# A first load that begins with one 2 KB descriptor per DMA engine instead of eight

## The chip, the cores and the metric

The kernel runs on one core of a Trainium2 chip. The metric is the device time of one execution in microseconds (us), taken as the median of several executions. All times within a trace count from the start of its span; the time of an execution is about 1.8 us longer than the span. An execution counts as slow when it is over 1.5% above the fastest of the same kernel.

## The reference

Each of the 32 x 3 images of 256 x 256 float32 values is turned by 180 degrees. Seen as a row of 65,536 numbers, an image is simply reversed:

```
x: (32, 3, 256, 256) float32
return np.rot90(x, k=2, axes=(-2, -1))
```

25.17 MB are read and 25.17 MB are written; nothing is calculated.

## The kernel before

The 96 images are handled in three groups of 32 images, one for each of the buffers A, Bt and Ct in SBUF, the memory of the core with its 128 partitions. Each image takes four partitions, so a load is 128 rows of 64 KB (E = 16,384 numbers). DVE, the vector engine, reverses the rows in place, in pieces of J = 2048 columns by way of a buffer T; the store puts the four rows of an image in reverse order. N = 512 columns are 2 KB; the first 2 KB of a row are called a strip here. All transfers are issued from SP, the sync engine, so they stand in one queue, from which 16 DMA engines take their rows. At the end of its share of a load each engine writes to the load's semaphore, a counter for which the next user waits; the last of these writes is the load's landing.

```python
# ... sizes, views, buffers, copy() on DVE and back(), the columns in reverse ...
def load(t, g, lo=0, hi=E):
    nc.sync.dma_start(out=t[:, lo:hi], in_=x4[g][:, lo:hi])

def store(t, g):
    nc.sync.dma_start(out=o4[g][:, ::-1, :], in_=t[:, :])

def inside(t):
    for lo in range(0, E // 2, J):
        hi = E - lo - J
        copy(T[:, :], back(t, hi, hi + J))
        copy(t[:, hi:hi + J], back(t, lo, lo + J))
        copy(t[:, lo:lo + J], T[:, :])

load(A, 0, 0, N)      # 128 strips of 2 KB
load(A, 0, N, E)      # 128 rows of 62 KB
load(Bt, 1)           # 128 rows of 64 KB
load(Ct, 2)
for g, t in enumerate((A, Bt, Ct)):
    inside(t)
    store(t, g)
# ... launch on one core ...
```

## Time and profile before

| what | value |
|---|---|
| time, median of 3 first runs | 122.92 us (122.82 to 123.0) |
| span of the profiled run | 121.1 us |
| DVE busy | 44.2 us |
| DMA packets' time, share of 16 engines | 97.4% |
| traffic | 50.33 MB, 416 GB/s over the span |

The lines themselves are shown and read in the prediction. The trace also records every single packet with its start, duration and size. A packet of 64 KB is one row; where this document speaks of an engine's rows, the numbers come from these records, as the mean of the 16 engines. The records do not name the engine: the n-th rows of all engines are the n-th sixteen long packets in order of their starts.

### The profile page before, as it was taken

What the parts mean: (1) busy time and instruction counts of PE and PEld (TensorE: products, weight loads), DVE (VectorE), ACT (ScalarE), POOL (GpSimd) and SP (SyncE); (2) the same over time, 40 slices, a digit from 0 to 9 for tenths busy, and PEclk for the clock granted to TensorE, in tenths of its full rate; (3) what the DMA queues carried; (4) which work ended last, traced back from release to release, by engine and by line L of the source; (5) the groups of instructions that cost most, each with busy time, mean ns of one, the idle gap of its engine ahead of it and who ended that gap; (6) DMA issues with size and microseconds to landing.
All of it is one profiled execution on the core that took longest, in us unless ns stands there. A gap on an engine that the chain in (4) does not pass through costs nothing.

```text
span 121.1 us, 94 instructions
## 1 busy us (share of the span) xinstructions
DVE 44.2 (36%) x36; POOL 0.2 (0%) x4
## 2 busy tenths in 40 slices
DVE  0000000599994199998039999600000000000000
POOL 0000000000000000000000000000000000000000
DMA  9977987897799879978989977997799779977980
GB/s 359 399 336 336 650 356 336 346 693 346 346 411 628 346 346 476 563 346 346 346 346 476 563 346 346 563 476 346 346 584 455 346 346 606 433 346 346 671 368 0
DMA packets 1008, 50.33 MB, mean 416 GB/s; under 512 B 112, under 2 KB 112, under 8 KB 240
## 3 DMA queue, kind: packets, MB, share of 16 engines
q1 hardware_dynamic: 1008, 50.33, 97.4%
HBM read 25.17 MB, written 25.17 MB: 416 GB/s over the span
## 4 chain that ended last, share of the span: by engine, by line
DMA 33%; DVE 25%; another core or an unknown queue 4%; issue 1%; SPq 1%; DVEq 0%
DMA Bt<-in_x_dram 33%; DVE T L53 8%; DVE Ct L53 8%; DVE Bt L53 8%; SPq L56 1%; DVEq L53 0%
## 5 line engine op out<-in xcount | busy, mean ns | idle before, releaser
L53 DVE COPY T<-A 128x2048 f32<-128x2048 f32 x4 | 4.9, 1227 | 22.7 <-DMA A<-in_x_dram 22.6
L53 DVE COPY T<-Ct 128x2048 f32<-128x2048 f32 x4 | 4.9, 1227 | 5.4 <-DMA Ct<-in_x_dram 5.3
L53 DVE COPY T<-Bt 128x2048 f32<-128x2048 f32 x4 | 4.9, 1227 | 4.4 <-DMA Bt<-in_x_dram 4.3
L53 DVE COPY Bt<-T 128x2048 f32<-128x2048 f32 x4 | 4.9, 1227 | 0.1
L53 DVE COPY A<-T 128x2048 f32<-128x2048 f32 x4 | 4.9, 1227 | 0.1
L53 DVE COPY Ct<-Ct 128x2048 f32<-128x2048 f32 x4 | 4.9, 1227 | 0.1
L53 DVE COPY Bt<-Bt 128x2048 f32<-128x2048 f32 x4 | 4.9, 1227 | 0.1
L53 DVE COPY A<-A 128x2048 f32<-128x2048 f32 x4 | 4.9, 1227 | 0.1
L53 DVE COPY Ct<-T 128x2048 f32<-128x2048 f32 x4 | 4.9, 1227 | 0.1
L89 POOL MEMSET const-bfloat16-1.0<- 128x1 bf16 x1 | 0.1, 101 | 0.0
L89 POOL MEMSET const-uint8-127<- 128x1 uint8 x1 | 0.1, 101 | 0.0
L89 POOL MEMSET const-float32-0.0<- 128x1 f32 x1 | 0.1, 98 | 0.2 <-issue 0.2
L89 POOL MEMSET const-float32-1.0<- 128x1 f32 x1 | 0.1, 98 | 0.0
## 6 DMA issues: line engine op xcount, KB each, us to landing
A<-in_x_dram SPq DMA_DIRECT2D x1, 7936.0 KB, 21.4
A<-in_x_dram SPq DMA_DIRECT2D x1, 256.0 KB, 2.8
Bt<-in_x_dram SPq DMA_DIRECT2D x1, 40.3
Ct<-in_x_dram SPq DMA_DIRECT2D x1, 60.3
out_dram<-A SPq DMA_DIRECT2D x1, 43.9
out_dram<-Bt SPq DMA_DIRECT2D x1, 43.8
out_dram<-Ct SPq DMA_DIRECT2D x1, 42.7
```

The source lines that it names most:

```text
L53: tc.keep_in_program_order(nc.vector.tensor_copy(out=dst, in_=src))
L56: nc.sync.dma_start(out=t[:, lo:hi], in_=x4[g][:, lo:hi])
L89: nc = _bacc.Bacc("TRN2", target_bir_lowering=False, num_devices=1)
```

## The change

The strip in front exists to set the engines to work early. The change makes it as small as it can be, one descriptor for each of the 16 engines, so that the long rows can begin sooner. The other 112 strips follow behind the long rows.

```diff
-    def load(t, g, lo=0, hi=E):
-        nc.sync.dma_start(out=t[:, lo:hi], in_=x4[g][:, lo:hi])
+    def load(t, g, lo=0, hi=E, i=0, j=P):
+        nc.sync.dma_start(out=t[i:j, lo:hi], in_=x4[g][i:j, lo:hi])
...
-    load(A, 0, 0, N)
+    load(A, 0, 0, N, 0, 16)
     load(A, 0, N, E)
+    load(A, 0, 0, N, 16, P)
     load(Bt, 1)
     load(Ct, 2)
```

## The prediction

> **What bounds the kernel now.** I read the page from the top: the busy shares first, then the queue's share, then the chain that ended last, and then, since the change touches only the first microseconds of the transfers, the windows and the single packets there. The page of the kernel before:
>
> ```profile
> span 121.1 us, 94 instructions
> ...
> DVE 44.2 (36%) x36; POOL 0.2 (0%) x4
> ...
> DMA packets 1008, 50.33 MB, mean 416 GB/s; under 512 B 112, under 2 KB 112, under 8 KB 240
> ## 3 DMA queue, kind: packets, MB, share of 16 engines
> q1 hardware_dynamic: 1008, 50.33, 97.4%
> ...
> DMA 33%; DVE 25%; another core or an unknown queue 4%; issue 1%; SPq 1%; DVEq 0%
> ```
>
> The only compute engine that works, DVE, is busy for 44.2 of 121.1 us. The one queue keeps the 16 DMA engines busy for 97.4% of the span. The chain that ended last names DVE for 25%, which misleads: it follows semaphores and not the place in the queue. The issues show this:
>
> ```profile
> A<-in_x_dram SPq DMA_DIRECT2D x1, 7936.0 KB, 21.4
> A<-in_x_dram SPq DMA_DIRECT2D x1, 256.0 KB, 2.8
> ...
> out_dram<-A SPq DMA_DIRECT2D x1, 43.9
> out_dram<-Bt SPq DMA_DIRECT2D x1, 43.8
> ```
>
> Each load or store of 8 MB alone takes about 19.3 us (8.39 MB at 435 GB/s), yet a store lands 43.9 us after its issue: it stands some 24 us behind the loads ahead of it. The store of A is issued at 37.76 us (timeline) and the load of Ct has landed only at about 62.4 us, when DVE begins on Ct. So the vector work has more than 20 us of slack, and the span is: time to the first packet, plus what each DMA engine has to move, plus the end. The windows (us from the start of the span, busy DVE and POOL, clock, DMA share, GB/s) give the same by stage:
>
> ```profile
> 0.00:1.70 1.70, 0.00 (x0) 0.20 (x4) 1.00 0.00 0
> 1.70:2.70 1.00, 0.00 (x0) 0.00 (x0) 1.00 0.75 184
> 2.70:21.80 19.10, 0.00 (x0) 0.00 (x0) 1.00 1.01 430
> 21.80:41.10 19.30, 14.72 (x12) 0.00 (x0) 1.00 1.00 435
> ...
> 119.50:121.10 1.60, 0.00 (x0) 0.00 (x0) 1.00 0.01 0
> ```
>
> Nothing moves until 1.7 us; for a microsecond the engines move the 2 KB strips at 184 GB/s; from there on they run at 430 to 435 GB/s. Only the second row can be improved by this change.
>
> **What the Trainium skill says.** (1) "DMA: Bandwidth & Descriptors", section "Where 436 GB/s comes from", puts the ceiling of the 16 engines together at 435 GB/s; the window from 21.8 to 41.1 us shows 435, so it agrees, and no change of order can speed the bulk. (2) The same page, "Why a DMA increments its semaphore by 16 and not by 1", says that a DMA from the SP queue takes the largest number of engines up to 16 that divides the slowest dimension. So 16 rows go one to each engine, and 112 rows seven to each. Before, every load has 128 rows, and the trace shows 16 landings on each semaphore; 112 rows no run has shown yet. (3) The same page, "Queues, rings and completion order": each engine takes its descriptors in ring order. The packet records agree: on each engine the 62 KB rows follow the strip with no gap. (4) "SBUF — State Buffer", "Door 1: The DMA port swizzle", has 16 ports, shared by eight partitions each in fours, so seven consecutive rows lie on two or three ports. Whether that costs anything is not visible before.
>
> **The change part by part.** The bytes stay the same: 50.33 MB, so 3.146 MB for each of 16 engines. Per engine the records of single packets show for the kernel before: eight strips of 2 KB at 0.084 us each when settled (the first takes 0.08 to 0.62 us, the start-up), a semaphore write of 0.009 us, eight rows of 62 KB at 2.342 us, and forty rows of 64 KB at 2.418 us.
>
> *Removed from the head.* Seven of eight strips, 7 x 0.084 = 0.59 us per engine. The first 62 KB rows now start at 2.71 to 3.18 us, mean 2.95.
>
> *What then sets the start of the 62 KB rows.* They need their descriptors. The first load is issued at 0.73 us and its first packet starts at 1.75 us, so 1.02 us later; the 16 engines start one after another, from 1.75 to about 2.27. The first issue takes 0.39 us and the second one starts at 1.18 us. If an issue of 16 rows takes as long as one of 128, the second load's descriptors reach the first engine at 1.18 + 1.02 = 2.20 us and the last at about 2.7, with a mean of about 2.45 us. The first strip, with its start-up, ends at about 2.1 to 2.4, so it is hidden behind that. The rows thus start 2.95 - 2.45 = 0.50 us earlier.
>
> *Added.* The seven strips come back behind the 62 KB rows, at about 21.3 us: 7 x 0.084 = 0.59 us, and one more semaphore write, 0.01 us. The third issue on SP, some 0.4 us, runs while the engines have 18 us of work queued: off the path. So the sum is -0.50 + 0.60 = +0.10 us per engine. The strip was never lost time: the engines worked through it while the next load's descriptors were being made, and now they may wait some tenths for them.
>
> *Ports.* Before, the packets of one engine and those of another did not hinder each other (2.342 us for nearly every row). With seven rows in one block, several engines write to the same port. From the port map I worked out, with the 0.08 us per row and the starts as they are scattered now, 0 to 0.6 us more per engine, depending on the engine; since the end is set by the slowest engine, I take +0.2 us as an estimate from that page, about half of the full effect.
>
> *DVE.* Its first copy needs only the second load's columns and may start 0.5 us earlier; the second copy reads the strip and waits for the third load, at about 22.7 us; before, it started at 23.89 (timeline). That is far inside the slack of 20 us.
>
> The sum: 122.92 + 0.10 + 0.20 - 0.10 (the scatter of the starts, 0.5 us, may shrink with one descriptor per engine, which helps the engine that ends last) = 123.12, so **about 123.1 us**.
>
> **The rivals.** *A, the head is really shortened:* if issuing 16 rows takes much less than 0.39 us, the second issue starts up to 0.3 us sooner, all the engines are on long rows at about 2.2 us, and the start-up is overlapped. For it speaks the rate of 184 GB/s in that microsecond; against it that all of the lost part is (1.00 - 0.42) us and that much of it is the very first packet's latency, which stays. This gives 122.5 to 122.8. *B, the ports or the uneven rows bind:* if the seven rows collide fully, or if the engines get unlike numbers of rows (for instance by partition groups, so that engines that hold rows 0 to 15 get four and others eight), the slowest engine loses 0.5 us or more: 123.4 to 123.7. Even spread by groups would not lose much if the 16 rows were spread so too, since the sums agree. *C, all 112 rows on a single engine:* 112 x 0.084 = 9.4 us on one engine, so 131 us. The rule of point (2) and the 128-row loads speak against it. *D, a DVE wait becomes the bound:* it would take more than 20 us of delay, and nothing here makes that.
>
> **Range and chances.** From A's middle (122.6) to B's upper end (123.7), with the three runs of before between 122.82 and 123.0: 122.6 to 123.7. Two per cent is 2.46 us. Nothing in the head can give that: the whole time from 1.7 to 2.7 us is worth 1 us. Faster by over 2%: 0.01. Slower: only C or a bad stall, 0.02. Within: 0.97.
>
> **What would show it.** In the packets: the first 62 KB rows start at about 2.45 us on average (right), at 2.2 or less (A), or later than 2.8 (the issue costs more than I think). The second load's landing comes some 0.5 us earlier, at about 22.1; the third's at about 22.7 to 22.9. The strips at 21.3 us take 0.084 us each if the ports don't matter, and well over 0.1 if they do. The first copy of Bt starts at 42.05 us before, which is the cleanest sum of all this: I expect 42.1 to 42.4, and the same shift at the end. The issue durations on SP show whether 16 rows are cheaper. I am wrong if the end moves while the start of Bt does not, since then something in the stores has changed, or if 112 rows don't spread evenly.

## The result, and the profile after

The changed kernel takes 123.09 us (122.98 to 123.27, 6 runs), the kernel before 122.92 us (122.81 to 123.0, 6 runs). The ratio is 1.0017, with a 95% interval of 1.0004 to 1.003. Ratios here are the mean time of one kernel's fast runs over that of the other's fast runs of the same rounds, so they are not quite the ratio of the medians. In a second job the changed kernel took 123.04 us and the ratio was 1.0006 (0.9989 to 1.0022). So the change costs at most some tenths of a microsecond.

The page of the changed kernel, the lines that answer to those of before:

```profile
span 121.3 us, 96 instructions
...
DVE 44.2 (36%) x36; POOL 0.2 (0%) x4
...
DMA packets 1024, 50.33 MB, mean 415 GB/s; under 512 B 128, under 2 KB 128, under 8 KB 256
...
q1 hardware_dynamic: 1024, 50.33, 97.2%
...
A<-in_x_dram SPq DMA_DIRECT2D x1, 7936.0 KB, 21.5
A<-in_x_dram SPq DMA_DIRECT2D x1, 224.0 KB, 21.8
A<-in_x_dram SPq DMA_DIRECT2D x1, 32.0 KB, 1.9
```

The same bytes, the same work on DVE, and 16 packets more: one more semaphore write on each engine. The load of 7936 KB lands 21.5 us after its issue, and 21.4 us before: the long rows, which were to gain half a microsecond, do not arrive sooner.

The windows at the head show that they do start sooner. Columns: window in us, its length, DVE and POOL busy, clock, DMA share, GB/s. A packet counts in the window in which it starts, so a high figure marks where the long rows start. The kernel before:

```profile
2.50:2.70 0.20, 0.00 (x0) 0.00 (x0) 1.00 1.02 399
2.70:2.90 0.20, 0.00 (x0) 0.00 (x0) 1.00 2.53 963
2.90:3.10 0.20, 0.00 (x0) 0.00 (x0) 1.00 10.57 4188
```

The changed kernel:

```profile
1.90:2.10 0.20, 0.00 (x0) 0.00 (x0) 1.00 0.34 41
2.10:2.30 0.20, 0.00 (x0) 0.00 (x0) 1.00 5.91 1905
2.30:2.50 0.20, 0.00 (x0) 0.00 (x0) 1.00 7.73 2540
```

The mass of the starts moves from about 3.0 us to about 2.3 us. The timeline, with the first copy out of each buffer, shows what came of it (start, duration, operation, and what ended DVE's idle time). The kernel before:

```profile
22.63 1.23 DVE L53 COPY T<-A 128x2048 f32<-128x2048 f32 x1 [22.63 <-DMA A<-in_x_dram]
...
42.05 1.23 DVE L53 COPY T<-Bt 128x2048 f32<-128x2048 f32 x1 [4.32 <-DMA Bt<-in_x_dram]
...
62.46 1.23 DVE L53 COPY T<-Ct 128x2048 f32<-128x2048 f32 x1 [5.31 <-DMA Ct<-in_x_dram]
```

The changed kernel:

```profile
0.73 1.33 SPq L57 DMA_DIRECT2D A<-in_x_dram  x3
...
22.66 1.23 DVE L54 COPY T<-A 128x2048 f32<-128x2048 f32 x1 [22.66 <-DMA A<-in_x_dram]
...
42.74 1.23 DVE L54 COPY T<-Bt 128x2048 f32<-128x2048 f32 x1 [4.98 <-DMA Bt<-in_x_dram]
...
62.62 1.23 DVE L54 COPY T<-Ct 128x2048 f32<-128x2048 f32 x1 [4.77 <-DMA Ct<-in_x_dram]
```

Bt arrives 0.69 us later, but Ct only 0.16 us later, and the end moves by as much. Something between 42 and 62 us gives half a microsecond back. The packet records, as means over the 16 engines in us, say where:

| event | before | after | difference |
|---|---|---|---|
| first 62 KB row starts | 2.95 | 2.37 | -0.59 |
| it takes | 2.56 | 3.08 | +0.52 |
| it ends | 5.52 | 5.45 | -0.07 |
| last 62 KB row of A ends | 21.96 | 21.85 | -0.12 |
| first row of Bt starts | 21.97 | 22.43 | +0.46 |
| it takes | 2.42 | 2.63 | +0.21 |
| last row of Ct starts | 58.21 | 58.92 | +0.71 |
| it takes | 3.55 | 2.99 | -0.56 |
| last row of Ct ends | 61.76 | 61.91 | +0.15 |
| last row of the last store ends | 119.72 | 119.87 | +0.15 |

The differences are those of the unrounded means. There are two surprises. The early start is lost in the first long row itself. And the last row of the loads holds a pause, 1.13 us beyond the settled 2.418 us, on all 16 engines at once; after the change it is 0.57 us. In the kernel before it lowers the rate in two windows, which the prediction's table leaves out:

```profile
41.10:61.00 19.90, 14.72 (x12) 0.00 (x0) 1.00 1.03 422
61.00:80.70 19.70, 14.72 (x12) 0.00 (x0) 1.00 0.98 426
```

### The profile page after: what moved, and what is told of

It is laid out like the page before. It is cut to its first block, busy times and chain, and to the rows that moved or that the text cites. A ratio compares the mean times of both kernels' runs of the same rounds, so it can differ in the third digit from the quotient of the medians.

```text
span 121.3 us, 96 instructions
## 1 busy us (share of the span) xinstructions
DVE 44.2 (36%) x36; POOL 0.2 (0%) x4
## 4 chain that ended last, share of the span: by engine, by line
DMA 33%; DVE 24%; another core or an unknown queue 4%; SPq 1%; issue 1%; DVEq 0%
DMA Bt<-in_x_dram 33%; DVE T L54 8%; DVE Ct L54 8%; DVE Bt L54 8%; SPq L57 1%; DVEq L54 0%
## 5 line engine op out<-in xcount | busy, mean ns | idle before, releaser
L54 DVE COPY T<-A 128x2048 f32<-128x2048 f32 x4 | 4.9, 1227 | 22.8 <-DMA A<-in_x_dram 22.7
## 6 DMA issues: line engine op xcount, KB each, us to landing
A<-in_x_dram SPq DMA_DIRECT2D x1, 7936.0 KB, 21.5
```

Of the source, the lines that this page charges most:

```text
L54: tc.keep_in_program_order(nc.vector.tensor_copy(out=dst, in_=src))
```

## The experiments

I ran twelve kernels in four jobs, each with five rounds beside the kernel before, which gave four to six executions of each. The edits are given against one of the two kernels. In the table, "pause" is the mean time that the last row of the loads takes beyond 2.418 us; the rows are means of the 16 engines in the profiled run; times are medians, with the ratio to the kernel before of the same job and its interval. The rows come from one trace of each kernel.

| run | time | ratio | first long row takes | Bt starts | first Bt row takes | pause | last row ends |
|---|---|---|---|---|---|---|---|
| again_before | 122.95 | 1.0011 (0.9983 to 1.0039) | 2.58 | 21.97 | 2.42 | 1.01 | 119.59 |
| again_after | 123.04 | 1.0006 (0.9989 to 1.0022) | 3.10 | 22.53 | 2.70 | 0.46 | 119.92 |
| head_only | 122.72 | 0.9982 (0.9964 to 1.0000) | 3.09 | 21.88 | 2.42 | 0.89 | 119.38 |
| tail_only | 123.23 | 1.0017 (1.0001 to 1.0033) | 2.58 | 22.55 | 2.58 | 0.78 | 120.14 |
| late_128 | 123.65 | 1.0055 (1.0037 to 1.0073) | 3.09 | 22.48 | 2.42 | 0.92 | 119.99 |
| no_strip | 123.03 | 1.0011 (0.9992 to 1.0030) | 3.14 | 21.93 | 2.42 | 1.17 | 119.79 |
| no_dve | 122.95 | 0.9997 (0.9984 to 1.0011) | 2.52 | 21.92 | 2.43 | 1.11 | 119.65 |
| swap_groups | 122.90 | 0.9993 (0.9980 to 1.0007) | 2.53 | 21.93 | 2.42 | 1.36 | 119.90 |
| gap | 122.90 | 0.9992 (0.9974 to 1.0010) | 2.57 | 21.90 | 2.42 | 1.16 | 119.68 |
| gap2 | 125.67 | 1.0218 (1.0201 to 1.0236) | 2.66 | 23.95 | 3.01 | 1.17 | 122.34 |
| gap07 | 129.20 | 1.0501 (1.0484 to 1.0519) | 2.69 | 27.36 | 3.17 | 1.07 | 125.81 |

(In "gap" the second load was that of Ct and the last that of Bt; its columns are those of the second and of the last load. no_strip has 64 KB in its first rows, for which 2.42 is the settled time.) The twelfth run, act_stores, comes last.

**Both kernels once more: again_before, again_after.** No edit.

> The kernel before once more, for a second trace of it. In the first trace the last row of the Ct load took 1.13 us longer than the other rows on the mean of the 16 DMA engines (starts 58.1 to 58.5 us). Theory 1, this pause belongs to the kernel (to the turn from loads to stores): it comes again with 1.0 to 1.3 us. Theory 2, it is chance of one execution: it is anywhere between 0 and 2 us, or elsewhere. Time 122.9 us for both.

> The changed kernel once more. In its first trace the mean pause in the last Ct row was only 0.57 us, and the first 62 KB rows took 0.74 us more than settled ones. Theory 1 (belongs to the kernel): both come again within 0.15 us. Theory 2 (chance): the pause is as likely 1.1 as 0.6 us. Time 123.1 us for both.

The pause came again with 1.01 us and 0.46 us, and the first long rows took 2.58 and 3.10 us. So both come again with their kernel and are not chance of one trace (expected were 1.0 to 1.3 us, and 0.57 and 0.74 us within 0.15). One execution of the kernel before ran at 123.85 us, so the interval of this job is wide.

**The head alone: head_only.** The result is wrong: 112 strips are missing.

```diff
     load(A, 0, 0, N, 0, 16)
     load(A, 0, N, E)
-    load(A, 0, 0, N, 16, P)
+    copy(A[:, 0:N], A[:, N:2 * N])
```

> The first half of the change alone: the 16-row strip, then the long rows; the other 112 strips are never loaded, DVE fills those columns with a copy of the next ones (the result is wrong on purpose). It moves 0.23 MB less, 0.59 us per engine. Theory 1, the earlier start of the long rows is eaten by their own start-up: the last-but-one landing of A stays at a mean of 22.3 us, as in both kernels, and Bt lands at a mean of 41.5 to 41.7 us; nothing of the 0.59 us is seen there. Rival, the start-up is a matter of the clock time or of chance: A and Bt land 0.4 to 0.6 us earlier, 41.1 to 41.3. Time: if the pause at the turn to the stores takes up shifts, 122.8 to 122.9 either way; if it doesn't, 122.8 under theory 1 and 122.4 under the rival.

```profile
41.95 1.23 DVE L54 COPY T<-Bt 128x2048 f32<-128x2048 f32 x1 [3.89 <-DMA Bt<-in_x_dram]
...
62.19 1.23 DVE L54 COPY T<-Ct 128x2048 f32<-128x2048 f32 x1 [5.14 <-DMA Ct<-in_x_dram]
```

These timeline lines are of head_only. Although it moves seven strips (0.59 us) less on each engine, DVE starts on Bt only 0.10 us sooner than in the kernel before (42.05 us), and the landing of Bt has a mean of 41.57 us, within the 41.5 to 41.7 expected. So the earlier start of the long rows buys a tenth of a microsecond at most, whatever comes later. The time, 122.72 us, lies a little below what theory 1 allowed; the rival's 122.4 is missed as well.

**The tail alone: tail_only.** The strips of 112 rows are loaded a second time.

```diff
-    load(A, 0, 0, N, 0, 16)
+    load(A, 0, 0, N)
     load(A, 0, N, E)
     load(A, 0, 0, N, 16, P)
```

> The second half alone: all 128 strips first, as before, then the long rows, then the strips of 112 rows once more (needless bytes, 0.23 MB more). Theory 1: Bt lands 0.80 us later than before (7 x 0.084 for the strips and 0.21 us for a slow first Bt row), mean 42.4 to 42.5 us, and the pause in the last Ct row falls from 1.13 to about 0.55 us, so that the end moves only by 0.2 us: 123.1 us. Rival, the pause shrank in the changed kernel for a reason of the head or by chance: it stays 1.1 us here and the end moves by the whole 0.8 us: 123.7 us.

```profile
42.76 1.23 DVE L54 COPY T<-Bt 128x2048 f32<-128x2048 f32 x1 [4.97 <-DMA Bt<-in_x_dram]
...
62.81 1.23 DVE L54 COPY T<-Ct 128x2048 f32<-128x2048 f32 x1 [4.95 <-DMA Ct<-in_x_dram]
```

In tail_only DVE starts 0.71 us late on Bt and 0.35 us late on Ct. The landing of Bt has a mean of 42.54 us, 0.88 us after that of before (41.66). The pause fell, to 0.78 us, but not to 0.55. So the late strips alone cost all of the delay at Bt, and they alone already bring a part of the refund. The time of 123.23 us lies nearer to theory 1 than to the rival's 123.7.

**The ports: late_128.** The third load brings all 128 rows, so that it is spread over the engines as every other load is.

```diff
     load(A, 0, 0, N, 0, 16)
     load(A, 0, N, E)
-    load(A, 0, 0, N, 16, P)
+    load(A, 0, 0, N)
```

> The changed kernel, but the third load brings the strips of all 128 rows (rows 0 to 15 a second time)[...]; one strip more per engine, 0.084 us. Theory 1, ports: in the changed kernel the blocks of seven rows made engines hinder one another, which stretched the last strips to as much as 0.14 us and the first Bt rows by 0.21 to 0.28 us; here the strips take 0.084 us throughout, the first Bt rows less than 0.05 us more than settled ones, and Bt lands at a mean of 42.3 us. Rival, any burst of short strips before long rows costs that: 0.2 us on the first Bt rows again, and Bt lands at 42.5 to 42.7 us. Time 123.0 to 123.2 us under both.

All 128 late strips took 0.084 us, where the 112 of the changed kernel took 0.0866 us on the mean and up to 0.140 (0.0914 and 0.132 in the repetition); the first Bt rows took 2.42 us, where they took 2.63 and 2.70. The landing of Bt had a mean of 42.20 us (42.48 in the changed kernel). So the layout of the block of 112 rows does slow the engines, and short strips as such do not. But the time went the other way than all expectations: 123.65 us, half a microsecond over the changed kernel, of which the eighth strip explains 0.08. The profiled execution was the fastest of its six, at 123.3 us; its pause was 0.92 us, and what the slower executions had in addition no trace shows. The smoother late load did not get the refund:

```profile
42.61 1.23 DVE L54 COPY T<-Bt 128x2048 f32<-128x2048 f32 x1 [4.99 <-DMA Bt<-in_x_dram]
...
62.77 1.23 DVE L54 COPY T<-Ct 128x2048 f32<-128x2048 f32 x1 [5.06 <-DMA Ct<-in_x_dram]
```

In late_128 DVE starts on Bt sooner than in the changed kernel (42.74 us) and on Ct later (62.62 us there).

**No strip: no_strip.**

```diff
-    load(A, 0, 0, N)
-    load(A, 0, N, E)
+    load(A, 0)
```

> No strip at all: the load of A in one piece of 64 KB rows. Theory 1, the start-up is paid in the first packets whatever their size: the first long rows take about 0.6 us longer than settled ones, A lands at a mean of about 22.2 us (22.30 with the strip) and the time is 122.8 to 122.95 us. Rival, the strip warms the transfers up cheaply and a start on long rows costs more: first rows 1.0 us or more too long, A lands at 22.5 us or later and the time is over 123.1 us.

The first rows took 3.14 us, 0.73 us more than settled ones, and A landed at 22.28 us. The time was 123.03 us, a little over theory 1's 122.95 and under the rival's 123.1: the strip of before, and the one after, are worth nothing that this measurement can tell. The first long row takes longer than a settled one, which is called the start-up here: by 0.73 us with nothing in front, 0.74 us behind one strip per engine, 0.22 us behind eight. With eight strips in front, part of it falls on them (the first of an engine took up to 0.62 us), and the row follows them without a gap. Behind one strip the engines had come to rest again: in the changed kernel the strips end at 2.01 us on the mean and the rows start at 2.37 us.

**What the pause is: no_dve, swap_groups.** no_dve drops the reversal (wrong), swap_groups exchanges the first and third group of images.

```diff
 no_dve:
     for g, t in enumerate((A, Bt, Ct)):
-        inside(t)
         store(t, g)
 swap_groups:
-    load(A, 0, 0, N)
-    load(A, 0, N, E)
+    load(A, 2, 0, N)
+    load(A, 2, N, E)
...
-    load(Ct, 2)
-    for g, t in enumerate((A, Bt, Ct)):
+    load(Ct, 0)
+    for g, t in ((2, A), (1, Bt), (0, Ct)):
```

> The kernel before without any vector work (wrong result on purpose): each store is issued as soon as its load has landed, at about 22, 42 and 62 us. Question: what is the pause of 1.0 to 1.1 us in the last Ct row, on all engines at once, just after the store of Bt has been issued (57.2 us). Theory 1, the turn from loads to stores itself: the pause stays at 58 to 61 us, 0.9 to 1.1 us, time 122.9 us. Rival, it is tied to the issue of a store or to the vector work: it disappears at 58 us or moves to 42 us; if it disappears, the time falls by about 1 us to 121.9 us.

> The kernel before with the first and third group of images exchanged, so the last load reads and the first store writes other addresses. Theory 1, the pause belongs to the turn from loads to stores, not to addresses: again 1.0 to 1.1 us in the last row of the last load, time 122.9 us. Rival, it belongs to the addresses of the last rows of group 2: it moves to the end of the first load, 20 to 22 us, or changes by over 0.4 us.

Without vector work the stores are issued at other times; the lines of no_dve's timeline:

```profile
22.55 0.62 SPq L60 DMA_DIRECT2D out_dram<-A  x1
...
41.83 0.55 SPq L60 DMA_DIRECT2D out_dram<-Bt  x1
```

There is no issue near 58 us any more, and no copy, yet the pause is there: 1.11 us in the rows that start at 58.0 to 58.4 us. With the groups exchanged it is 1.36 us, in the last load again. So it stays with the turn from loads to stores and is not tied to DVE, to an issue or to the addresses; nor to a time of the execution, for in gap07 below it comes in rows that start at 64.1 to 64.7 us. What makes it, no run shows. (The trace of swap_groups is of its slowest execution, 123.2 us, so the pause varies by some tenths from one execution to the next.)

**Is lost time refunded at the turn: gap, gap2, gap07.** Up to here it looked as if any time lost before the turn shortened the pause. A gap without bytes tests this. In gap the load of Bt waits for a tiny copy behind A:

```diff
     load(A, 0, N, E)
+    tc.keep_in_program_order(nc.vector.memset(Bt[:, 0:J], 0.0))
+    copy(Bt[:, 0:1], A[:, E - 1:E])
     load(Bt, 1)
```

> The kernel before, with a gap without any bytes put into the queue on purpose: the load of Bt waits for one tiny vector copy that waits for A, so it is issued at about 22.8 us, its packets start at about 23.8 to 24.3 instead of 21.9 to 22.3 us, and each DMA engine stands idle for about 2.0 us. So far, time that the engines lost to stalls before the turn to the stores (0.83 to 1.75 us) and the pause in the last Ct row (1.36 to 0.46 us) have always made a sum of 1.9 to 2.2 us. Theory 1, lost time is given back at the turn as long as there is pause left: the pause falls from 1.1 to about 0 us and the end moves by only 0.8 to 1.1 us: 123.7 to 124.1 us. Rival, only certain stalls (ports, start-up) shorten the pause, or the sum was chance: the pause stays near 1.1 us and the end moves by the full gap: 124.9 us.

This run failed as a test: the scheduler issued the load of Ct first, at 1.64 us, so there was no gap. It only shows that with Bt as the last load the pause stays with the last load (1.16 us). gap2 makes both loads wait and keeps their order, and gap07 has a chain of memsets instead, meant for a shorter gap:

```diff
+    copy(Bt[:, 0:1], A[:, E - 1:E])              # gap2
+    copy(Ct[:, 0:1], A[:, E - 1:E])              # gap2
+    for w in [J] * 11 + [N]:                     # gap07 instead
+        nc.vector.memset(Bt[:, 0:w], 0.0)        # (kept in program order)
     load(Bt, 1)                                  # issues kept in order
     load(Ct, 2)
```

> The gap once more, as the earlier run of this kind issued the load of Ct first and so had no gap: now both later loads wait for tiny vector copies behind A and are issued from about 22.9 us on in the order Bt, Ct. Each DMA engine stands idle for about 1.9 us without moving a byte. Theory 1, time lost before the turn is given back at the turn as long as there is pause left: the pause in the last Ct row falls from 1.1 to about 0 us and the end moves by 0.8 to 1.1 us: 123.7 to 124.1 us. Rival, only engines that hinder each other shorten the pause, not idle time: the pause stays at 0.9 to 1.2 us and the end moves by the full gap: 124.7 to 125.0 us.

> The same with a smaller gap: Bt and Ct wait for a chain of DVE memsets of Bt that ends at about 21.4 us, so the packets of Bt start at about 22.5 to 23.0 us instead of 21.9 to 22.3, some 0.7 us later, as late as in the changed kernel with its strips. Theory 1: the pause falls to about 0.5 us and the end moves by 0.0 to 0.3 us: 122.9 to 123.2 us. Rival: the pause stays near 1.1 us and the end moves by 0.7 us: 123.6 us.

The windows of gap2 show a real gap, in which no packet starts, and the timeline shows what became of it:

```profile
22.40:23.60 1.20, 1.02 (x3) 0.00 (x0) 1.00 0.00 0
23.60:24.40 0.80, 0.77 (x2) 0.00 (x0) 1.00 3.76 1311
```

```profile
44.67 1.23 DVE L54 COPY T<-Bt 128x2048 f32<-128x2048 f32 x1 [6.87 <-DMA Bt<-in_x_dram]
...
65.10 1.23 DVE L54 COPY T<-Ct 128x2048 f32<-128x2048 f32 x1 [5.33 <-DMA Ct<-in_x_dram]
```

DVE starts 2.62 us late on Bt in gap2 and 2.64 us late on Ct: nothing is refunded, and the pause is 1.17 us. The delay is more than the rival's 1.9 us, since 0.59 us of start-up in the first Bt rows come on top of 2.05 us of idle time; so the time, 125.67 us, is over its 125.0 as well. In gap07 the memsets took longer than I reckoned, so that the gap was 5.4 us instead of 0.7; again the pause stayed, at 1.07 us. The theory that any lost time is refunded has fallen. Of the two theories the rival is left, that only engines hindering one another shorten the pause; no run shows how they would. The two runs show one more thing: after a gap the first long rows again take 3.01 and 3.17 us instead of 2.42. The start-up cost of a long row behind idle engines, 0.6 to 0.75 us, is not tied to the beginning of the kernel.

**A candidate to beat both: act_stores.** The stores are issued from ACT, so that they need not wait behind the loads.

```diff
-        nc.sync.dma_start(out=o4[g][:, ::-1, :], in_=t[:, :])
+        nc.scalar.dma_start(out=o4[g][:, ::-1, :], in_=t[:, :])
```

> The kernel before with its three stores issued from ACT, whose ring is another one on the same engines: the store of A then no longer stands behind the whole load of Ct but takes turns with it from about 38.8 us on. A candidate to beat both. Theory 1, the pause comes with the one turn from loads to stores, and with both kinds in flight at once it vanishes or is hidden: up to 1 us faster, 121.9 to 122.4 us. Rival, the debt is paid anyway, or taking turns costs more than it saves: 122.9 us or more; the load of Ct lands later, at about 80 us, DVE starts on Ct later and the store of Ct still follows without a gap, since that of Bt keeps the engines busy to about 100 us.

It took 129.48 us in the one execution that counts as fast, and 131.5 to 132.7 us in five that count as slow (they are over 1.5% above it; no ratio is given). That is 5% over the kernel before in the same job (122.97 us), even with the fast one. Its trace, of a slow execution, has the two rings taking turns:

```profile
q1 hardware_dynamic: 576, 25.17, 48.6%
q10 hardware_dynamic: 432, 25.17, 45.6%
```

Its rows were stretched by 0.1 to 0.9 us on the mean again and again while both were in flight, instead of once. A second cost stands in the same trace: DVE could begin on Ct only at 90.99 us, and the store of Ct was issued so late that the engines stood idle for 1.3 us on the mean between 103 and 108 us, where the expectation had it follow without a gap:

```profile
106.12 0.55 ACTq L60 DMA_DIRECT2D out_dram<-Ct  x1
```

As this is a slow execution, I do not take the two for the whole cause. No kernel here with a right result is faster than the kernel before by more than the noise.

## Why the prediction was right or wrong

The predicted time was right, 123.1 against 123.09 us, and so was the sign. That the sum came so close is luck: a gain of 0.50 us, of which 0.07 came, and a refund of 0.56 us that the prediction did not have nearly cancelled.

- **What bounds the kernel.** Right. DVE's work moved and was even dropped (no_dve), and the time stayed at 122.95 us.
- **When the long rows start.** Right. The issue of 16 rows took 0.393 us and that of 128 rows 0.387, the second issue started at 1.18 us in both kernels, and the long rows started at 2.37 us on the mean (2.45 predicted). Rival A, a cheaper issue, was wrong.
- **"The rows thus start 0.50 us earlier", taken as a gain of 0.50 us.** This step failed. The start came 0.59 us sooner and the end of the same row only 0.07 us, for the row took 0.74 us more than a settled one, not 0.22 us. The prediction knew the start-up of the strips, but let it disappear behind the wait for descriptors. head_only and no_strip show that the first rows pay it instead. Nor did the -0.10 us for the scatter come: the rows' starts spread over 0.47 us before and 0.46 after. The landing of the second load, predicted at 22.1 us, stayed at 22.64 us (22.61 before).
- **The strips come back at the end of A, 0.60 us.** Right: the first row of Bt starts 0.58 us later against the end of A's last long row (+0.46 and -0.12), seven strips and a semaphore write. Their load landed at 23.44 us, though, and not at 22.7 to 22.9.
- **The ports, +0.20 us.** The size was right (0.21 us in the first Bt row, 0.28 in the repetition, 0.16 in tail_only); that it is "about half" of an effect of up to 0.6 us is a slip, as it is a third. That the layout of the block is the cause, late_128 shows; that it works through the ports is not shown, nor that an engine's seven rows lie together, as the records name neither engine nor partition. The cost fell less on the strips, of which only the last were over 0.1 us, than on the rows behind them.
- **The start of Bt as "the cleanest sum of all this".** Wrong: 42.74 us, not 42.1 to 42.4, and the end did not move by the same amount. The two costs above and the missing gain sum to about 0.7 us there.
- **The pause at the turn from loads to stores.** The prediction did not have it, although the trace of the kernel before showed it: 1.13 us in the last row of each engine. "From there on they run at 430 to 435 GB/s" is a wrong reading: the lines that it left out of its table have 422 and 426 (shown with the result). After the change it is 0.57 us, which hides the failed step. Why it shortens is not settled. The three runs with the block of seven strips per engine have the shortest ones (0.46, 0.57, 0.78 us). Two with the 16-row head and without the block have 0.89 and 0.92, and all the others 1.01 to 1.36. So, with one trace of each run, the pause goes with the change's parts, and most with the layout that slows the engines; idle time (gap2, gap07) does not shorten it, nor do late strips without the block (late_128 against head_only). By what the engines differ from 22 us on to the turn at 58 us, which would have to carry this, no run shows.
- **Rivals B, C and D.** All engines took part in the 112-row load: its semaphore has 16 landings, as after 16 and 128 rows, and the first engine to finish spent 0.56 us on its strips, seven times 0.080. So what the prediction took from the Trainium skill, "DMA: Bandwidth & Descriptors", section "Why a DMA increments its semaphore by 16 and not by 1", holds here; so does the ceiling of its section "Where 436 GB/s comes from", as the bulk ran at 435 GB/s. C and D did not occur. The slowing that B feared did, without its time.

## What to carry to other kernels

A transfer that starts sooner is worth only what its end gains, so compare landings and not starts: the first long packet of an idle engine took 0.6 to 0.75 us longer here wherever it stood. Where a load is split by rows, test whether the block slows what follows: the 112 rows here made the next rows 0.16 to 0.28 us longer, and 128 rows did not. Do not add up a delay to the end before looking for a later pause that may take part of it. A predicted total that comes true proves none of its terms; check each at its own place in the trace.

## What the Trainium skill lacked or had wrong

- "DMA: Bandwidth & Descriptors" has latencies of a first byte and of a round trip, but no page that I read gives the cost of the first long packets of all engines together: 0.73 us (no_strip), 0.74 us (after one strip each), 0.59 and 0.75 us (after a gap in mid-kernel), against 0.22 us behind eight strips.
- No page that I read tells of the pause at the turn from loads to stores in one queue: 1.01 to 1.36 us in the kernels with the 128-row head or none and no late strips.
- "SBUF — State Buffer", "Door 1: The DMA port swizzle", has the map, and the bandwidth of a transfer that reaches few ports, but no price for engines that share ports within one load: strips of up to 0.140 us instead of 0.084, and 0.16 to 0.28 us on the next 64 KB rows. late_128 does not contradict the map; that it is the ports, and not something else in the layout, no run shows. Which rows an engine gets of a 112-row load, I found on no page.
- "DMA: Bandwidth & Descriptors", "Issuing engines are not separate DMA queues", says that issuing from several engines only saves issue time. Here the stores from ACT, in flight together with loads from SP, made the kernel at least 6.5 us slower (129.48 against 122.97); in the one trace, of a slow execution, 1.3 us of the loss were idle time before the last store.
